# Head of the Strassen stage in written order, and one decay product behind the next projection

## The chip, the core and the metric

One core of a Trainium2 chip runs the whole program: TensorE (PE, with its weight loads as PEld), VectorE (DVE), ScalarE (ACT), GpSimd (POOL) and SyncE (SP), which issues the transfers. The metric is the device time of one execution in microseconds (us), lower is better, as the median of several runs.

## The reference

Two layers; each is a SwiGLU block, a mixer, and a second SwiGLU block, every one between two RMSNorms with a residual. There are 512 tokens, a width of 1024, a hidden width of 2816, all in float32.

```python
def swiglu_ffn(h, w_gate, w_up, w_down):
    return (jax.nn.silu(h @ w_gate) * (h @ w_up)) @ w_down

# inside the mixer, gated linear attention in chunks of 64 tokens
decay_to_end = lax.cumsum(la_c, axis=2, reverse=True) - la_c
chunk_decay = jnp.exp(jnp.sum(la_c, axis=2))
k_dec = to_chunks(k) * jnp.exp(decay_to_end)
```

The rest of the mixer (stick-breaking attention, a causal convolution, sigmoid gates, two output projections) is not touched by the change.

## The kernel before

**Precision.** A float32 operand is split into a high part (`whi`, `xh`: a rounded copy by ACT) and a low part (`wlo`, `xl`: the difference by DVE); a product is three matmuls, high by high, high by low and low by high. `split` and `load_w` do that for activations and weights. The order in which these helpers' instructions stand on ACT and DVE is left to a planner, which places each as soon as it expects it to be ready. `keep_in_program_order` pins an instruction behind the one written before it for the same engine. All matmuls and transposes are pinned.

**One SwiGLU block** (`ffn`, four times in the program: two in each layer) has 22 tiles of 128 hidden columns. Tiles 0 and 1 are computed token by token: `pf` holds gate and up of one block of 128 tokens, `ht` is their product, and four `ht` are transposed (`pth`) into `hid[0]` and `hid[1]`. Tile 2 is the classical tile: `pg` and `pu` are 24 matmuls each, then `hid[2]` is silu(`pg`) (ACT, L477) times `pu` (DVE, L478). Tiles 3 to 21 are computed by `block_tiles`, called the Strassen stage here: gate and up columns are taken together as a 2 by 2 block matrix, with seven products per tile instead of eight.

**Forms and operands.** The seven products take activations in seven forms: B11, B21, B22 are slices of `xh`/`xl`; T1 to T4 are sums over tokens that `Forms.arrive` makes and `Forms.finish` splits (L306 to L312). The weight side of each product is an operand that `prepare(g)` makes from the raw tile of the Strassen stage (sums on DVE, a copy to `whi` on ACT, and `low` for `wlo` on DVE, mostly for two products at a time). `product(g)` issues its 12 matmuls into bank A, B or C; `taken` and `summed` take the results out. `AHEAD = 6`: the loop runs from g = -6, and prepares the operand of product g + 6 in round g. Everything that `block_tiles` puts on ACT and DVE is pinned.

**Order before.** `ffn` writes the token tiles, `pg`, the transposes, all of `forms.finish()`, `pu`, the two instructions of `hid[2]` and then the whole of `block_tiles`. So the first pinned DVE instruction of `prepare(0)` stands behind the `hid[2]` product L478.

**Buffers.** `whi`/`wlo` have five slots; `raw` three tiles, each with room for one Strassen tile or two ordinary loads (`spare` holds the free half). The tag "s" has 14 slots: four `ht`, and four each for the split T3, T2 and T1 in the head.

**Decay.** `gla_decay` is a generator that the mixer moves on between convolution projections (`conv_in`, two projections each, `pa` and `pgl`). Its last part issues the `plam` matmuls, the exponential `lam` on ACT (L733), and for j = 0, 1 a product `pd` of 128x512 into one of the two banks of tag "pa". `plam` and the first `pd` fill these banks; the second `pd` takes the bank of `plam`.

Of the kernel before, what the change touches and what calls it, by code (L numbers as in the profile page):

```python
# [13 lines left out]
P = 128  # L14
# [27 lines left out]
def kernel(  # L42
# [21 lines left out]

    def mm(*a, **k):
        tc.keep_in_program_order(nc.tensor.matmul(*a, **k))  # L66

    def transpose(*a):
        tc.keep_in_program_order(nc.tensor.transpose(*a))
# [206 lines left out]
    class Forms:  # L276
# [24 lines left out]
                for j, n in enumerate(("T3", "T4")):  # L301
                    nc.vector.tensor_tensor(self.raw[n][c][:, :, tok], t2, first[j][:, k], op=ALU.add)

        def finish(self):
            for n, tag in (("T3", "s"), ("T2", "s"), ("T1", "s"), ("T4", "b")):
                hi = [slot(n + "h", F32R, tag).rearrange("p (k t) -> p k t", k=2) for c in range(2)]  # L306
                lo = [slot(n + "l", F32R, tag).rearrange("p (k t) -> p k t", k=2) for c in range(2)]
                for c in range(2):
                    split(hi[c], lo[c], self.raw[n][c])
                self.parts[n] = [(hi[k // 2][:, k % 2], lo[k // 2][:, k % 2]) for k in range(4)]  # L310
            for n, k0, t0 in (("B11", 0, 0), ("B21", 4, 0), ("B22", 4, 256)):
                self.parts[n] = [(xh[:, k0 + k, t0:t0 + 256], xl[:, k0 + k, t0:t0 + 256]) for k in range(4)]  # L312

    H0, H1 = slice(0, 256), slice(256, 512)

# [2 lines left out]
    PLACES = (0, 1, 0, 2, 4, 3, 2)  # L318
    AHEAD = 6

    def block_tiles(w0, w1, fs, forms, hid):

        pin = tc.keep_in_program_order
        copy = lambda o, i: pin(nc.scalar.copy(o, i))  # L324
        silu = lambda o, i: pin(nc.scalar.activation(o, i, AF.Silu))
        tt = lambda o, a, b, op: pin(nc.vector.tensor_tensor(o, a, b, op=op))  # L326
        add = lambda o, a, b: tt(o, a, b, ALU.add)
        sub = lambda o, a, b: tt(o, a, b, ALU.subtract)
        n = 7 * len(fs)
        raw, banks, cps, ring = {}, {}, {}, {}  # L330

        def load(u):
            r = wp.tile([P, 5, 512], F32, tag="raw", name="raw", bufs=3)
            for w, q0 in ((w0, 0), (w1, 1)):
                for j in range(2):
                    nc.sync.dma_start(r[:, q0 + 2 * j].rearrange("p (k c) -> p k c", c=P),
                                      w[j * 512:(j + 1) * 512, fs[u] * P:(fs[u] + 1) * P]
                                      .rearrange("(k p) c -> p k c", p=P))
            raw[u] = r

        def low(g0, g1):

            hi, lo = ring[g0 // 2]
            q0, q1 = PLACES[g0 % 7], PLACES[g1 % 7]
            r, h = raw[g0 // 7], g0 % 2
            if g0 == g1:
                sub(lo[:, h], r[:, q0], hi[:, h].bitcast(F32))
            elif q0 < q1:
                sub(lo, r[:, q0:q1 + 1:q1 - q0], hi.bitcast(F32))
            else:  # L350
                sub(lo[:, ::-1], r[:, q1:q0 + 1:q0 - q1], hi[:, ::-1].bitcast(F32))

        def prepare(g):

            u, j = divmod(g, 7)
            r = raw[u]
            if j == 0:
                add(r[:, 4], r[:, 1], r[:, 3])
                add(r[:, 1], r[:, 1], r[:, 0])
            if j == 2:  # L360
                add(r[:, 0], r[:, 4], r[:, 0])
            if j == 5:
                add(r[:, 2], r[:, 2], r[:, 0])
            if g % 2 == 0:
                ring[g // 2] = [wp.tile([P, 1024], F32R, tag=t, name=t).rearrange("p (f c) -> p f c", f=2)
                                for t in ("whi", "wlo")]
            copy(ring[g // 2][0][:, g % 2], r[:, PLACES[j]])
            if g % 2 and j:
                low(g - 1, g)
            elif g % 2 or j == 6:  # L370
                low(g, g)

        def product(g):
            u, j = divmod(g, 7)
            name, b = PRODUCTS[j]
            if j == 0:
                banks[u] = [bank(x) for x in "ABC"]
                cps[u] = gp.tile([P, D], F32, tag="g", name="cp")
            ps = banks[u][b][:, H0]
            hi, lo = (t[:, g % 2].rearrange("p (k c) -> p k c", c=P) for t in ring[g // 2])  # L380
            first = j in (0, 1, 3)
            for k, (fh, fl) in enumerate(forms.parts[name]):
                for m, (a, b_) in enumerate(((hi, fh), (hi, fl), (lo, fh))):
                    mm(ps, a[:, k], b_, start=(first and k == 0 and m == 0), stop=False, skip_group_check=True)

        def parts(u):
            cp = cps[u]
            return [cp[:, x * 256:(x + 1) * 256] for x in range(4)], hid[fs[u]], banks[u]

        def taken(g):  # L390

            u, j = divmod(g, 7)
            (p1, p7, u2, u4), h, (A, B, C) = parts(u)
            if j == 0:
                copy(p1, A[:, H0])
            if j == 1:
                copy(p7, C[:, H0])
            if j == 2:
                copy(u2, A[:, H0])
            if j == 4:  # L400
                copy(u4, A[:, H0])
            if j == 6:
                silu(h[:, H0], h[:, H0])
                silu(h[:, H1], A[:, H0])

        def summed(g):

            u, j = divmod(g, 7)
            (p1, p7, u2, u4), h, (A, B, C) = parts(u)
            if j == 3:  # L410
                add(h[:, H0], B[:, H0], p1)
            if j == 5:
                sub(u2, C[:, H0], u2)
                sub(u4, p7, u4)
            if j == 6:
                tt(h, cps[u][:, 512:1024], h, ALU.mult)

        for g in range(-AHEAD, n + 1):
            f = g + AHEAD
            if f % 7 == 0 and f < n:  # L420
                if f == 0:
                    load(0)
                if f // 7 + 1 < len(fs):
                    load(f // 7 + 1)
            if 0 < g:
                taken(g - 1)
            if 0 <= g < n:
                product(g)
            if f < n:
                prepare(f)  # L430
            if 0 < g:
                summed(g - 1)
# [8 lines left out]
    def ffn(wg, wu, wd, weights, forms, arrive, finish, upcoming, early, late, begin):  # L441

        if begin is None:
            wgt, wut = weights
        else:
            wgt = load_kcols(wg, 0, 256)
            begin(0)
            wut = load_kcols(wu, 0, 256)
            begin(1)
            arrive[0]()  # L450
        hk = []
        for i in range(NT):
            pf = bank("pf", "pb")
            mm_tok(pf[:, 0:256], i, wgt)
            if i + 1 < NT:
                arrive[i + 1]()
            mm_tok(pf[:, 256:512], i, wut, first=False)
            h = slot("ht", tag="s")
            nc.scalar.activation(h[:, 0:256], pf[:, 0:256], AF.Silu)
            nc.vector.tensor_tensor(h[:, 0:256], pf[:, 256:512], h[:, 0:256], op=ALU.mult)  # L460
            hk.append(h)
        hid = [None] * NF

        def turn(f):
            pt = bank("pth", "pa")
            for i in range(NT):
                transpose(pt[:, i * P:(i + 1) * P], hk[i][:, f * P:(f + 1) * P], ident)
            hid[f] = slot("hid", tag="q")
            nc.scalar.copy(hid[f], pt)

        pg = proj_cols(wg, 2 * P, "pg")
        turn(0)
        turn(1)
        forms.finish()
        pu = proj_cols(wu, 2 * P, "pu")
        hid[2] = slot("hid")
        nc.scalar.activation(hid[2], pg, AF.Silu)  # L477
        nc.vector.tensor_tensor(hid[2], pu, hid[2], op=ALU.mult)  # L478
        spare.clear()
        for f in range(3, NF):  # L480
            hid[f] = slot("hid", tag="t" if f < 18 else "q")
        block_tiles(wg, wu, list(range(3, NF)), forms, hid)
        late()

        def stat(f):
            sh, sl = slot("sh", F32R, "s"), slot("sl", F32R, "s")
            split(sh, sl, hid[f])
            return sh, sl

        return out_proj(wd, NF, stat, TAIL, finish, upcoming, early)  # L490


    def mixer(l, wv, arrive, finish, upcoming, early):
# [138 lines left out]
        ys = []  # L632
        taps = []

        def conv_in(c):
            pa = proj_cols(W, C_A + c * P, "pa")
            pg = proj_cols(W, C_G + c * P, "pgl")
            sg = slot("sgl", tag="s")
            nc.scalar.activation(sg, pg, AF.Sigmoid)
# [62 lines left out]
        def gla_decay(lrt):  # L702
# [31 lines left out]
            for j in range(2):  # L734
# [2 lines left out]
                e = slot("ge")  # L737
                nc.scalar.activation(e, pd, AF.Exp)
                nc.vector.tensor_tensor(gk[j], gk[j], e, op=ALU.mult)
            yield  # L740

        def gla_q():
            for c in range(2):
# [59 lines left out]
        conv_in(2)  # L803
        next(decay[0])
        conv_taps(10)
        conv_in(3)
        wr = load_kcols(W, C_GR, 512)
        conv_taps(4)

# [267 lines left out]
```

## Time and profile before

| | before |
|---|---|
| median of 3 runs | 2400.56 us (2398.08 to 2402.35) |
| profiled execution, own time | 2397.77 us |
| its span, first to last instruction | 2396.1 us |
| mean granted TensorE clock | 0.993 |
| PE busy | 2360.0 us (98%) |
| DVE / ACT / POOL busy | 1631.2 / 1118.0 / 175.9 us |

The profile is one execution. A matmul's end is modelled, so the intervals between starts are safer than durations. "Idle before" a row is the time for which its engine stood still, and the name behind the arrow is what ended it. The granted clock is 1.00 at 2.4 GHz and 0.50 at 1.2 GHz.

### The profile page before, as it was taken

The numbers are of one execution on the slowest core, as the hardware profiler recorded it, in microseconds if no ns is written. First come the engines' busy times: TensorE is split into PE (matmuls) and PEld (weight loads), VectorE is DVE, ScalarE is ACT, GpSimd is POOL, SyncE is SP. The second block draws the span as 40 slices with busy tenths as digits, with TensorE's granted clock in tenths as the row PEclk, the third lists the DMA queues.
The fourth block names the chain that finished last, engine by engine and source line by source line (L and its number), as shares of the span: only waits on it lengthen the run. The fifth ranks groups of instructions, "written<-read, shape, count | busy, mean of one in ns | idle before, by whom it ended". The sixth has DMA issues, their size and how long they took to land.

```text
span 2396.1 us, 35810 instructions
## 1 busy us (share of the span) xinstructions
PE 2360.0 (98%) x14264; PEld 2104.1 (88%) x14264; DVE 1631.2 (68%) x2329; ACT 1118.0 (47%) x2148; POOL 175.9 (7%) x287
## 2 busy tenths in 40 slices
PE   7999999999999999999999999999999999999998
PEld 7999888887888889998889998888878888899987
DVE  6888436858965378884378884378599644788833
ACT  5555425644323355563355563366333334455622
POOL 0000001201011100000000000012010211000000
PEclk9999999999999999999999999999999999999999
DMA  5333323231333223334223333241313332333421
GB/s 151 106 107 106 141 88 99 70 93 53 107 88 105 80 66 106 104 103 146 76 71 107 106 113 134 71 116 53 110 53 106 88 104 64 88 106 105 134 101 40
DMA packets 307159, 231.74 MB, mean 97 GB/s; under 512 B 11722, under 2 KB 284140, under 8 KB 306992
## 3 DMA queue, kind: packets, MB, share of 16 engines
q1 hardware_dynamic: 306992, 229.46, 32.2%
q8 instruction: 111, 1.82, 0.3%
q14 instruction: 56, 0.46, 0.1%
HBM read 227.32 MB, written 2.10 MB: 96 GB/s over the span
## 4 chain that ended last, share of the span: by engine, by line
PE 96%; DVE 2%; ACT 1%; issue 0%; POOL 0%; DMA 0%; SPq 0%; DVEq 0%; POOLq 0%; ACTq 0%
PE o L66 23%; PE A L66 18%; PE gate L66 11%; PE C L66 9%; PE pb L66 5%; PE B L66 5%; PE pf L66 4%; PE pa L66 2%; PE gr L66 2%; PE q L66 2%; PE gv L66 2%; PE k L66 2%; PE pgl L66 2%; PE pv L66 2%; PE pu L66 1%; PE gk L66 1%
## 5 line engine op out<-in xcount | busy, mean ns | idle before, releaser
L106 DVE TENSOR_TENSOR wlo<-raw,whi 128x1024 fp32r<-128x1024 f32 (+1 forms) x266 | 332.9, 1257 | 227.2 <-ACT whi L105 220.0
L105 ACT CAST whi<-raw 128x1024 fp32r<-128x1024 f32 (+1 forms) x266 | 278.1, 1046 | 391.8 <-PE gate L66 122.6
L326 DVE TENSOR_TENSOR wlo<-raw,whi 128x1024 fp32r<-128x1024 f32 (+1 forms) x304 | 330.5, 1088 | 117.7 <-ACT whi L324 117.5
L324 ACT CAST whi<-raw 128x512 fp32r<-128x512 f32 x532 | 314.2, 619 | 187.3 <-DVE raw L326 187.3
L66 PE MATMUL o<-whi,sh 128*128 128x512 f32 x704 | 274.2, 389 | 0.0
L66 PE MATMUL o<-wlo,sh 128*128 128x512 f32 x704 | 273.9, 389 | 0.0
L66 PE MATMUL o<-whi,sl 128*128 128x512 f32 x704 | 273.9, 389 | 0.0
L326 DVE TENSOR_TENSOR raw<-raw 128x512 f32<-128x512 f32 x304 | 209.2, 688 | 6.6
L106 DVE TENSOR_TENSOR sl<-hid,sh 128x512 fp32r<-128x512 f32 x88 | 60.0, 689 | 192.3 <-ACT sh L105 192.3
L66 PE MATMUL A<-xh,wlo 128*128 128x256 f32 x608 | 174.8, 288 | 15.1 <-DVE wlo L326 15.1
L66 PE MATMUL A<-xl,whi 128*128 128x256 f32 x608 | 173.6, 286 | 0.0
L66 PE MATMUL A<-xh,whi 128*128 128x256 f32 x608 | 173.6, 286 | 0.0
L667 DVE SCALAR_TENSOR_TENSOR y<-u,cw,y 128x511 f32<-128x511 f32 (+14 forms) x240 | 164.1, 743 | 0.0
L105 ACT CAST sh<-hid 128x512 fp32r<-128x512 f32 x88 | 54.4, 622 | 230.5 <-PE o L66 230.5
L66 PEld LDWEIGHTS o<-whi,sl 128*128 128x128 f32 x704 | 132.1, 188 | 27.4
L66 PEld LDWEIGHTS o<-wlo,sh 128*128 128x128 f32 x704 | 132.2, 188 | 27.3
L66 PEld LDWEIGHTS o<-whi,sh 128*128 128x128 f32 x704 | 132.2, 188 | 27.2
L66 PE MATMUL gate<-xh,whi 128*128 128x512 f32 x384 | 151.3, 394 | 0.0
L66 PE MATMUL gate<-xl,whi 128*128 128x512 f32 x384 | 149.6, 390 | 0.0
L66 PE MATMUL gate<-xh,wlo 128*128 128x512 f32 x384 | 149.5, 389 | 0.0
L193 POOL TENSOR_TENSOR rs<-ms,mhalf 128x1 f32<-128x1 f32 x48 | 30.9, 644 | 1480.2 <-DVE ms L191 1480.2
L66 PEld LDWEIGHTS A<-xh,wlo 128*128 128x128 f32 x608 | 118.8, 195 | 15.9 <-DVE wlo L326 15.9
(278 smaller groups left out, 6241.4 us busy)
## 6 DMA issues: line engine op xcount, KB each, us to landing
raw<-in_w_in_dram SPq DMA_DIRECT2D x108, 512.0 KB, 4.2
raw<-in_ffn_w_down_dram SPq DMA_DIRECT2D x88, 512.0 KB, 4.4
raw<-in_ffn_w_gate_dram SPq DMA_DIRECT2D x152, 256.0 KB, 3.4
raw<-in_ffn_w_up_dram SPq DMA_DIRECT2D x152, 256.0 KB, 4.5
raw<-in_w_branch_dram SPq DMA_DIRECT2D x24, 512.0 KB, 3.8
raw<-in_w_out_dram SPq DMA_DIRECT2D x16, 512.0 KB, 4.1
raw<-in_ffn_w_gate_dram SPq DMA_DIRECT2D x12, 512.0 KB, 5.4
raw<-in_ffn_w_up_dram SPq DMA_DIRECT2D x12, 512.0 KB, 4.0
```

What stands on the lines that cost most here:

```text
L66: tc.keep_in_program_order(nc.tensor.matmul(*a, **k))
L105: nc.scalar.copy(hi, src)
L106: nc.vector.tensor_tensor(lo, src, hi.bitcast(F32), op=ALU.subtract)
L193: nc.gpsimd.tensor_tensor(rs, ms, mhalf[:, 0:1], op=ALU.pow)
L324: copy = lambda o, i: pin(nc.scalar.copy(o, i))
L326: tt = lambda o, a, b, op: pin(nc.vector.tensor_tensor(o, a, b, op=op))
L667: nc.vector.scalar_tensor_tensor(y[:, back:], u[:, :S - back], cw[:, c, j:j + 1], y[:, back:], op0=ALU.mult, op1=ALU.add)
```

## The change

The forms, the token sums and the classical tile are no longer finished ahead of `block_tiles`, but inside its rounds, by a function `between(g)` that is called at the start of each round. `finish` splits one form at a time, with pinned instructions. The last `ht`, the loads of the classical tile's weights, `pg`, `pth` and `pu` keep their order on PE. In the mixer the generator yields after each `pd`, and `conv_in(3)` moves it on between its two projections.

```diff
-        def finish(self):
-            for n, tag in (("T3", "s"), ("T2", "s"), ("T1", "s"), ("T4", "b")):
...
-                for c in range(2):
-                    split(hi[c], lo[c], self.raw[n][c])
+        def finish(self, n):
+            tag = "b" if n == "T4" else "s"
...
+            for c in range(2):
+                pinned(nc.scalar.copy(hi[c], self.raw[n][c]))
+            for c in range(2):
+                pinned(nc.vector.tensor_tensor(lo[c], self.raw[n][c], hi[c].bitcast(F32), op=ALU.subtract))
...
         for g in range(-AHEAD, n + 1):
+            between(g)
             f = g + AHEAD
...
-        pg = proj_cols(wg, 2 * P, "pg")
-        turn(0)
-        turn(1)
-        forms.finish()
-        pu = proj_cols(wu, 2 * P, "pu")
-        hid[2] = slot("hid")
-        nc.scalar.activation(hid[2], pg, AF.Silu)
-        nc.vector.tensor_tensor(hid[2], pu, hid[2], op=ALU.mult)
+        def between(g):
+            if g == -6:
+                sides.append(load_cols(wg, 2 * P))
+                forms.finish("T3")
+            if g == -5:
+                silu_up(NT - 1, pf)
+                sides.append(load_cols(wu, 2 * P))
+                pg = bank("pg")
+                mm_cols(pg, *sides[0])
+                for f in range(2):
+                    pt = bank("pth", "pa")
+                    for i in range(NT):
+                        transpose(pt[:, i * P:(i + 1) * P], hk[i][:, f * P:(f + 1) * P], ident)
+                    pts.append(pt)
+                pu = bank("pu")
+                mm_cols(pu, *sides[1])
+                pts.extend((pg, pu))
+            if g == -4:
+                forms.finish("T2")
+            if g == -2:
+                forms.finish("T1")
+                for f in range(2):
+                    hid[f] = slot("hid", tag="q")
+                    pinned(nc.scalar.copy(hid[f], pts[f]))
+            if g == -1:
+                hid[2] = slot("hid")
+                pinned(nc.scalar.activation(hid[2], pts[2], AF.Silu))
+            if g == 0:
+                forms.finish("T4")
+            if g == 1:
+                pinned(nc.vector.tensor_tensor(hid[2], pts[3], hid[2], op=ALU.mult))
...
-        block_tiles(wg, wu, list(range(3, NF)), forms, hid)
+        sides = []
+        spare.clear()
+        block_tiles(wg, wu, list(range(3, NF)), forms, hid, between)
...
-        def conv_in(c):
+        def conv_in(c, mid=None):
             pa = proj_cols(W, C_A + c * P, "pa")
+            if mid is not None:
+                next(mid)
             pg = proj_cols(W, C_G + c * P, "pgl")
...
                 nc.vector.tensor_tensor(gk[j], gk[j], e, op=ALU.mult)
-            yield
+                yield
...
-        conv_in(3)
+        conv_in(3, decay[0])
```

## Rows read from the trace of the kernel before

**Rows 1.** The page: busy us (share) xinstructions, and granted clock in 40 slices.
```profile
PE 2360.0 (98%) x14264; PEld 2104.1 (88%) x14264; DVE 1631.2 (68%) x2329; ACT 1118.0 (47%) x2148; POOL 175.9 (7%) x287
...
PEclk9999999999999999999999999999999999999999
```

**Rows 2.** Waits of PE over the span: us in total, times, longest.
```profile
PE A L66 <- DVE wlo L326: 15.1, 4, 3.8
...
PE pd L66 <- ACT lam L733: 3.3, 2, 1.7
```

**Rows 3.** Chain that ended last, first head: start us, us, what.
```profile
46.60 5.47 PE pu L66 x24
...
52.10 0.04 DVE hid L478
...
52.70 0.69 DVE raw L326
...
54.80 1.24 DVE wlo L326
...
56.08 2.50 PE A L66 x10
```

**Rows 4.** Windows: six products in four heads, then steady: length, PE busy (x), clock, DMA.
```profile
51.90:66.92 15.02, 11.24 (x74) 0.77 0.24 67
884.89:899.92 15.03, 11.25 (x73) 0.77 0.25 70
1241.54:1256.56 15.02, 10.80 (x73) 0.89 0.24 69
2071.69:2087.08 15.39, 11.61 (x74) 0.78 0.24 69
77.00:85.64 8.64, 8.64 (x75) 1.00 0.39 108
```

**Rows 5.** Windows right behind the first head's wait and the first decay's.
```profile
56.08:61.27 5.19, 5.19 (x24) 0.50 0.00 0
...
553.83:559.61 5.78, 5.78 (x12) 0.50 0.00 0
```

**Rows 6.** Timeline of DVE, first head: start us, us, instruction, count, [idle before <-releaser].
```profile
34.38 1.42 DVE L302 TENSOR_TENSOR T<-T,xr 128x256 f32<-128x256 f32 x4
...
41.22 1.29 DVE L106 TENSOR_TENSOR T3l<-T,T3h 128x512 fp32r<-128x512 f32 x2
...
47.88 0.69 DVE L106 TENSOR_TENSOR T1l<-T,T1h 128x512 fp32r<-128x512 f32 x1 [3.56 <-ACT T1h L105]
```

**Rows 7.** Timeline of ACT, first head.
```profile
46.26 1.07 ACT L469 COPY hid<-pth 128x512 f32<-128x512 f32 x2
...
47.72 0.64 ACT L324 CAST whi<-raw 128x512 fp32r<-128x512 f32 x1
```

**Rows 8.** Timeline of SP, second SwiGLU: transfers of the first and third Strassen tiles.
```profile
849.59 0.92 SPq L336 DMA_DIRECT2D raw<-in_ffn_w_gate_dram  x2
...
871.31 0.92 SPq L336 DMA_DIRECT2D raw<-in_ffn_w_gate_dram  x2
```

**Rows 9.** Timeline of PE around the first decay.
```profile
549.36 1.84 PE L66 MATMUL plam<-indic,gm 128*128 128x2 f32 x16
551.06 1.10 PE L66 MATMUL pd<-gm,strict 128*128 128x512 f32 x2
553.83 2.07 PE L66 MATMUL pd<-gm,strict 128*128 128x512 f32 x2 [1.67 <-ACT lam L733]
```

**Rows 10.** Chain that ended last, ACT's part of the first decay.
```profile
553.59 0.19 ACT lam L733
```

**Rows 11.** Windows: one `pa` projection, then both decays from `plam` to `pgl`.
```profile
538.33:543.92 5.59, 5.59 (x26) 1.00 0.75 189
549.36:562.98 13.62, 11.95 (x45) 0.75 0.00 0
1738.86:1749.78 10.92, 9.25 (x45) 1.00 0.00 0
```

More of the change, by code (lines that the diff above doesn't have):

```diff
@@ L66, in mm @@
         tc.keep_in_program_order(nc.tensor.matmul(*a, **k))
+    pinned = tc.keep_in_program_order
     def transpose(*a):
@@ L302, in arrive, with form @@
                     nc.vector.tensor_tensor(self.raw[n][c][:, :, tok], t2, first[j][:, k], op=ALU.add)
-        def finish(self):
-            for n, tag in (("T3", "s"), ("T2", "s"), ("T1", "s"), ("T4", "b")):
-                hi = [slot(n + "h", F32R, tag).rearrange("p (k t) -> p k t", k=2) for c in range(2)]
-                lo = [slot(n + "l", F32R, tag).rearrange("p (k t) -> p k t", k=2) for c in range(2)]
-                for c in range(2):
-                    split(hi[c], lo[c], self.raw[n][c])
-                self.parts[n] = [(hi[k // 2][:, k % 2], lo[k // 2][:, k % 2]) for k in range(4)]
-            for n, k0, t0 in (("B11", 0, 0), ("B21", 4, 0), ("B22", 4, 256)):
+        def finish(self, n):
+            tag = "b" if n == "T4" else "s"
+            hi = [slot(n + "h", F32R, tag).rearrange("p (k t) -> p k t", k=2) for c in range(2)]
+            lo = [slot(n + "l", F32R, tag).rearrange("p (k t) -> p k t", k=2) for c in range(2)]
+            for c in range(2):
+                pinned(nc.scalar.copy(hi[c], self.raw[n][c]))
+            for c in range(2):
+                pinned(nc.vector.tensor_tensor(lo[c], self.raw[n][c], hi[c].bitcast(F32), op=ALU.subtract))
+            self.parts[n] = [(hi[k // 2][:, k % 2], lo[k // 2][:, k % 2]) for k in range(4)]
+        def form(self, n):
+            if n not in self.parts:
+                k0, t0 = {"B11": (0, 0), "B21": (4, 0), "B22": (4, 256)}[n]
                 self.parts[n] = [(xh[:, k0 + k, t0:t0 + 256], xl[:, k0 + k, t0:t0 + 256]) for k in range(4)]
+            return self.parts[n]
     H0, H1 = slice(0, 256), slice(256, 512)
@@ L319, with block_tiles @@
     AHEAD = 6
-    def block_tiles(w0, w1, fs, forms, hid):
-        pin = tc.keep_in_program_order
+    def block_tiles(w0, w1, fs, forms, hid, between):
+        pin = pinned
         copy = lambda o, i: pin(nc.scalar.copy(o, i))
@@ L381, in product @@
             first = j in (0, 1, 3)
-            for k, (fh, fl) in enumerate(forms.parts[name]):
+            for k, (fh, fl) in enumerate(forms.form(name)):
                 for m, (a, b_) in enumerate(((hi, fh), (hi, fl), (lo, fh))):
@@ L451, in ffn, with silu_up @@
         hk = []
+        hid = [None] * NF
+        def silu_up(i, pf):
+            h = slot("ht", tag="s")
+            nc.scalar.activation(h[:, 0:256], pf[:, 0:256], AF.Silu)
+            nc.vector.tensor_tensor(h[:, 0:256], pf[:, 256:512], h[:, 0:256], op=ALU.mult)
+            hk.append(h)
         for i in range(NT):
@@ L457, in ffn @@
             mm_tok(pf[:, 256:512], i, wut, first=False)
[L458 to L469, printed above, removed]
@@ L471, in ffn @@
-        pg = proj_cols(wg, 2 * P, "pg")
-        turn(0)
-        turn(1)
-        forms.finish()
-        pu = proj_cols(wu, 2 * P, "pu")
-        hid[2] = slot("hid")
-        nc.scalar.activation(hid[2], pg, AF.Silu)
-        nc.vector.tensor_tensor(hid[2], pu, hid[2], op=ALU.mult)
+            if i + 1 < NT:
+                silu_up(i, pf)
+        pts = []
+        def between(g):
[29 more added lines that the diff above has]
+                pinned(nc.vector.tensor_tensor(hid[2], pts[3], hid[2], op=ALU.mult))
+                for f in range(3, NF):
+                    hid[f] = slot("hid", tag="t" if f < 18 else "q")
@@ L479, in ffn @@
+        sides = []
         spare.clear()
-        for f in range(3, NF):
-            hid[f] = slot("hid", tag="t" if f < 18 else "q")
-        block_tiles(wg, wu, list(range(3, NF)), forms, hid)
+        block_tiles(wg, wu, list(range(3, NF)), forms, hid, between)
         late()
```

## The prediction

> **What bounds the kernel now.** I read the page first: PE is busy for 2360.0 us of the 2396.1 us span, and its granted clock shows 9 tenths or more in every slice, so slow stretches are short [rows 1]. Little can be won outside PE, and what can is where PE stands still or runs slow. So the second view is the waits of PE. Its two rows with several waits are 15.1 us in 4 waits for `wlo` and 3.3 us in 2 waits for `lam` [rows 2]; four is the number of SwiGLU blocks, two that of mixers. The third view, the chain of waits, shows what the first kind is made of. `pu` ends at 52.07; only then DVE can make the product `hid[2]` (52.10), and the sums on `raw` (52.70), the copy and `wlo` (54.80) follow one after the other; bank A resumes at 56.08 [rows 3]. The sums do not read `pu`. Their tile was loaded long before (in the second block its transfers went out at 849.59, 35 us ahead of the head at 884.89 [rows 4, 8]); they stand behind the `hid[2]` product because they are pinned to DVE's order. Fourth, I asked for windows: six products of 12 matmuls of 256 columns last 8.64 us in the steady stretch (6 x 1.44), but about 15 us in each head [rows 4], and the clock right behind the wait is 0.50, that is 1.2 GHz, after PE had stood still for 3.78 us [rows 5].
>
> **The change part by part: the heads.** No matmul is added or removed, and PE's order is kept. What leaves the path is the dependence of the first sums on `pu`. The price of a head is its window less 8.64: 15.02 - 8.64 = 6.38, then 6.39, 6.38 and 6.75, together 25.90 us [rows 4]. That holds the wait itself (4 x 3.78 = 15.1) and 10.8 us of slow clock and operands that come late behind it.
>
> What is late next? I put the new order on DVE, in times of the first head. T3 and T4 sums end at 34.38 + 1.42 = 35.8 [rows 6]. From then DVE has, in written order, T3l (1.29), two sums (0.7 each), the split of the `pu` weights (1.23), `low` of products 0 and 1 (1.23), T2l (1.29), a sum (0.7), `low` of 2 and 3 (1.23), the last `ht` (0.42): 8.8 us, durations of such instructions in the same timeline [rows 3, 6]. It would end near 44.6 if nothing held it; some 2 us go to waits for ACT's copies, so 47. `pu` ends at 52.07 [rows 3], so product 0 finds its operand some 5 us early or more.
>
> The next link is T1l. It needs two more slots of tag "s": four `ht`, eight for T3 and T2 and two for T1h are 14 of 14, so it waits for the transposes of `ht`. Before, the second T1l ran at 47.88, behind that same release, and the copies out of `pth` on ACT at 46.26 [rows 6, 7]. Behind T1l stand a sum and `low` of 4 and 5: 47.9 + 1.3 + 0.7 + 1.2 = 51.1. Product 4 starts at 51.9 + 4 x 1.44 = 57.7. Then T4l and `low` of 6: 51.1 + 2.0 = 53.1, against 60.5. So every operand has 6 us or more. ACT needs a copy of 0.6 us for each operand and form half, fewer than DVE's. I take the new wait at 0, with the full 25.9 us won; the cover is this lead, and if half of it were gone, the price is the second rival's.
>
> Of moved steps: the product `hid[2]` goes to round 1, behind `low` of 6, with nobody waiting for it until the output projection, a whole stage later. Its wait for `pu` at 52.07 is over by then; behind it in DVE's queue are the sums for product 7, due at 62. On SP, the `pu` weights are now written behind the loads of the first two Strassen tiles. In the second block, the first of these went out at 849.59 and the third, which waits for the `pu` split, at 871.31 [rows 8]; `pu`, which takes 5.5 us [rows 3], starts there at about 884.9 - 5.5 = 879.4 [rows 4]. Landing takes about 4 us, so even behind the second load the weights come in time: 0. The 16 form instructions, sums and copies are the same in number: 0.
>
> **The decay.** After `plam` and the first `pd` at 551.06, the second `pd` waits 1.67 us, because its bank is the one that ACT must read for `lam` first, at 553.59 [rows 9, 10]. Now 24 matmuls of `pa`, 5.59 us, stand between [rows 11]: from about 552.1 to 557.7, 4 us after `lam`. The wait goes: 2 x 1.67 = 3.34. In the first layer the clock fell to 0.50 for 5.78 us behind it [rows 5], in the second it did not: 13.62 - 10.92 = 2.70 more [rows 11]. Together 6.04 us. The second exponential and the product on `gk` come about 5 us later; `gk` of the second half is first read in the fifth chunk, behind four gate projections of 24 matmuls: 0. Built up instead from the parts (1.70 for `plam`, two `pd` of 1.03, 5.59), the pair of windows should be 9.35 each, a gain of 5.84, so the two ways agree within 0.2.
>
> **Sum.** 25.90 + 6.04 = 31.9 us. Against the profiled execution, 2397.77 - 31.9 = 2365.9. That execution was the shortest seen, 2.8 under the median, so the median after should be 2400.56 - 31.9 = 2368.6; I say 2368.5.
>
> **The rivals.**
> *The decay gives nothing back.* If the planner puts the late exponential where ACT is in the way of the next projection, 6.04 is lost again: 2374.6. For: ACT switches function tables around `lam`. Against: `lam` itself takes 0.19 us [rows 10], an exponential on 512 columns about as long as any copy of 512, 0.6 us, and the projection behind has its weights in five slots, loaded ahead. 5%.
> *Half the lead is gone.* One wait stays in each head, at product 2 or 4, of the size of the decay's: 1.67 and 2.70 for the clock, 4 x 4.37 = 17.5 kept: 2386.1. For: T1l hangs on a slot. Against: the 6 us computed above. 5%.
> *The wait was for a buffer.* The same wait of 3.78 us stands in four heads; were it a wait for a free `whi` slot, order would not help and only the decay would gain: 2400.56 - 6.04 = 2394.5. Against: the first operand's copy had its slot at 47.72, before `pu` ended [rows 7], and DVE ran its sums without a break from `hid[2]` on. The Trainium skill, "Perfetto Trace Analysis", section "Identifying Performance Opportunities", says that the same gap repeating on the engine that should be saturated can mean that there is no room for the next tile; here the rows speak for queue order instead. 5%.
> *Slower: DVE paces the head.* A pair of products takes PE 2.88 us, while DVE needs about 3.2 for it now that a form's split stands in the same chain (1.29 + 0.7 + 1.23). With the lead it does not matter. If the chain started only as `pu` ends, which takes a first link held by something that `pu` releases, each head would lose the old 6.4 and the four form splits, 4 x 1.29 = 5.2, which before lay in DVE's idle time: 4 x 5.2 - 6.0 = 14.8 slower, 2415. It turns slower than before when more than 1.5 us of splits a head lands behind `pu`. Against: T3's sums are there 16 us earlier. 3%.
>
> **How the numbers follow.** The forecast has 82%. Its own range is 2363 (the profile's 2365.9 less the 2.5 us between median and fastest run) to about 2373. With the first rival the range goes to 2378 and leaves out some 13%. A measurement can tell about 0.2%, 4.8 us, from no change. Forecast and the first two rivals are faster (92%); of the buffer case, at 6 us, 2 in 5 parts count as faster and 3 as the same; so 94, 3 and 3%.
>
> **What would show it.** After: no wait of bank A for `wlo` at a head, and windows of 8.6 us for the first six products at clock 1.00; the `hid[2]` product on DVE behind the seventh operand; T1l right behind the transposes; no wait for `lam`, and about 9.4 us from `plam` to `pgl` in both layers. Wrong would be a wait inside the first block, at product 2, 4 or 6, with DVE's T2l or T1l just ahead of it, or a late `pu`.

## The result and the profile after

The kernel after takes 2366.84 us (median of 4 runs, 2366.42 to 2367.24), the kernel before 2399.32 (4 runs, 2397.08 to 2402.35) beside it: a ratio of 0.9864 with a 95% interval of 0.9847 to 0.9881, 32.5 us or 1.4% less. Forecast were 2368.5 us, with a range of 2363 to 2378. The profiled executions differ by 2397.77 - 2367.24 = 30.5 us, their spans by 2396.1 - 2365.5 = 30.6, against the 31.9 of the prediction's sum.

The page of the kernel after, span and busy time:

```profile
span 2365.5 us, 35797 instructions
...
PE 2347.7 (99%) x14264; PEld 2094.3 (89%) x14264; DVE 1629.1 (69%) x2329; ACT 1117.9 (47%) x2148; POOL 181.1 (8%) x287
```

PE has the same 14264 matmuls, and is busy for 12.3 us less than in [rows 1]: that part of the gain had gone to slow clock, the rest to standing still. The waits of PE after (us in total, times, longest):

```profile
PE pt L71 <- DVE hn L210: 7.7, 1, 7.7
PE pf L66 <- ACT xh L107: 1.6, 1, 1.6
PE gate L66 <- DVE wlo L108: 1.3, 2, 0.6
PE pf L66 <- DVE xl L108: 0.8, 2, 0.6
```

Both rows of [rows 2] are gone. `pt` and `pf` wait at the start of the program, as before. One row is new: the first `gate` projection of each mixer waits 0.6 us for `wlo`.

The windows of the first six products in the four heads (length, PE busy (x instructions), granted clock, DMA share, GB/s), which answer to [rows 4]:

```profile
52.48:61.11 8.63, 8.63 (x74) 1.00 0.44 123
875.17:883.81 8.64, 8.64 (x73) 1.00 0.43 123
1225.13:1233.77 8.64, 8.64 (x73) 1.00 0.44 121
2047.90:2056.54 8.64, 8.64 (x74) 1.00 0.43 121
```

Each head runs at the steady pace from its first matmul and at full clock: 60.46 - 34.55 = 25.91 us less. For the decay I take windows from the start of `plam` to the start of `pu`, the first matmuls of the linear attention, behind the last projection of the convolution (there the moved `pd` is inside both times). First the kernel before, then after:

```profile
549.36:568.51 19.15, 17.48 (x69) 0.82 0.19 56
1738.86:1755.31 16.45, 14.78 (x69) 1.00 0.12 33
```

```profile
543.35:557.92 14.57, 14.57 (x69) 1.00 0.00 1
1716.06:1730.64 14.58, 14.58 (x70) 1.00 0.01 2
```

That is 35.60 - 29.15 = 6.45 us less. The rest of the balance: the two new waits at the gate, 1.3 us of standing, and the first head, which starts at 52.48 instead of 51.90, 0.6 later. The latter is no effect of the change: it arises between 16.9 and 18.3 us, where PE issued 14 matmuls in the execution before and 8 in the one after, and in a second execution of the kernel after the first head starts at 51.99. 25.91 + 6.45 - 1.26 - 0.58 = 30.5.

Last, the timeline of DVE and of ACT in the first head after (start us, us, instruction, count, [idle before <-releaser]):

```profile
40.30 1.22 DVE L336 TENSOR_TENSOR wlo<-raw,whi 128x1024 fp32r<-128x1024 f32 x1
...
46.96 1.29 DVE L314 TENSOR_TENSOR T1l<-T,T1h 128x512 fp32r<-128x512 f32 x2 [0.83 <-PE pth L71]
...
49.41 1.22 DVE L336 TENSOR_TENSOR wlo<-raw,whi 128x1024 fp32r<-128x1024 f32 x1 [0.56 <-ACT whi L334]
...
51.76 0.68 DVE L336 TENSOR_TENSOR wlo<-raw,whi 128x512 fp32r<-128x512 f32 x1
...
52.96 0.68 DVE L513 TENSOR_TENSOR hid<-pu,hid 128x512 f32<-128x512 f32 x1
```

```profile
50.30 0.64 ACT L334 CAST whi<-raw 128x512 fp32r<-128x512 f32 x1
50.82 0.64 ACT L107 CAST sh<-hid 128x512 fp32r<-128x512 f32 x1
54.11 0.37 ACT L334 COPY cp<-A 128x256 f32<-128x256 f32 x1 [2.65 <-PE A L66]
...
56.99 0.37 ACT L334 COPY cp<-A 128x256 f32<-128x256 f32 x1 [0.55 <-PE A L66]
```

`low` of products 0 and 1 is done at 41.5, 11 us ahead of product 0 at 52.48; the product with `pu` runs behind the seventh operand and holds up nobody. The rows to remember are the last two, ACT's copies of products 0 and 2 out of bank A. ACT stands idle for 2.65 us until PE has filled the bank for the first, and for 0.55 us before the second. Products 2 and 4, which need the emptied bank, start at 55.35 and 58.23, 0.87 us behind the end of each copy.

### The profile page after: what moved, and what is told of

The parts are those of the page before. It is cut to its first block, busy times and chain, and to the rows that moved or that the text cites. A ratio compares the mean times of both kernels' runs of the same rounds, so it can differ in the third digit from the quotient of the medians.

```text
span 2365.5 us, 35797 instructions
## 1 busy us (share of the span) xinstructions
PE 2347.7 (99%) x14264; PEld 2094.3 (89%) x14264; DVE 1629.1 (69%) x2329; ACT 1117.9 (47%) x2148; POOL 181.1 (8%) x287
## 3 DMA queue, kind: packets, MB, share of 16 engines
q1 hardware_dynamic: 306992, 229.46, 32.5%
## 5 line engine op out<-in xcount | busy, mean ns | idle before, releaser
L66 PEld LDWEIGHTS A<-xh,whi 128*128 128x128 f32 x608 | 116.7, 192 | 0.2
```

## The experiments

My theory: each head stood still only because its first sums stood behind the `hid[2]` product in DVE's order, and the new order has lead enough. The rivals: the forms have to be interleaved too; the wait was for a buffer; a wait stays inside the head. For the decay: the second `pd` waited for its bank. "Before" is the kernel before, run on the same chip as each experiment.

| kernel | median, us | runs from to | before |
|---|---|---|---|
| decay part alone | 2392.65 | 2391.98 to 2394.75 | 2398.44 |
| heads alone | 2372.47 | 2369.08 to 2373.71 | 2398.44 |
| before, `hid[2]` product moved alone | 2377.90 | 2376.12 to 2379.61 | 2398.44 |
| before, `pd` in other banks | 2393.98 | 2393.33 to 2394.42 | 2398.44 |
| after, `hid[2]` in round -3 | 2382.38 | 2382.01 to 2382.58 | 2399.50 |
| after, `hid[2]` in round -4 | 2398.31 | 2397.00 to 2399.39 | 2399.50 |
| after, all of tile 2 ahead of T3 | 2417.62 | 2415.99 to 2418.07 | 2399.50 |
| round -3, operands 5 and 6 later | 2389.88 | 2389.38 to 2391.57 | 2398.26 |
| `hid[2]` alone, operands 5 and 6 later | 2375.08 | 2374.79 to 2378.60 | 2398.26 |
| after, once more | 2366.73 | 2366.33 to 2367.08 | 2400.26 |
| after, four taps later | 2365.19 | 2364.95 to 2365.76 | 2399.50 |
| after, two taps later | 2365.47 | 2365.16 to 2365.55 | 2400.26 |

**Each part alone.** The two halves of the diff were applied one at a time.

> Only the decay part of the change, on the kernel before. By the sum of the prediction: no wait of PE for lam, 6.0 us less than the 2399.3 of before, 2393.3, perhaps 1.3 more if the two waits of 0.6 us for wlo at the first gate, which the trace of after shows, belong to this part (2394.6). Rival, the decay gives nothing back: 2399.

> Only the heads, the decay as before. By the sum: 25.9 us less, 2373.4, no wait of bank A, and the two waits for lam still there. If the two waits for wlo at the first gate belong to the heads, they are seen here too. Rival, the two parts overlap in what they win (a shared slow clock): then this run is under 2370.

Measured: 5.8 us less for the decay (ratio 0.9979, 0.9969 to 0.9988) and 26.0 less for the heads (0.9890, 0.9873 to 0.9906). Together 31.8, against 32.5 for both in one kernel: they add up, with no shared part that the two medians could show. The waits of PE, decay part alone, then heads alone:

```profile
PE A L66 <- DVE wlo L326: 15.1, 4, 3.8
...
PE gate L66 <- DVE wlo L106: 1.3, 2, 0.6
```

```profile
PE pd L66 <- ACT lam L770: 3.3, 2, 1.7
```

The new wait at the gate belongs to the decay part.

**The bank of `pd`.** This edit moves no instruction in the written program:

```diff
-                pd = bank("pd", "pa")
+                pd = bank("pd")
```

> The kernel before with the pd products in banks of the six of tag pb instead of the two of tag pa; order untouched. If the second pd waited for the bank that lam reads, the wait goes without any move: 2393.3 (6.0 less), possibly 2394.6. Rival, pd waits for ACT for another reason (ACT's exponential behind it): 2399 and the wait is still in the trace.

Measured: 4.5 us less (0.9983, 0.9974 to 0.9993), between the two values expected. PE has no wait for `lam` any more, and the waits of 0.6 us at the gate are there:

```profile
PE A L66 <- DVE wlo L326: 15.1, 4, 3.8
...
PE gate L66 <- DVE wlo L106: 1.3, 2, 0.6
```

So the second `pd` waited for the bank that ACT had yet to read, and a free bank takes the same wait away as the move. Its median is 1.3 us above that of the move. In the two profiled executions this is not in the stretches with the decay: from the first matmul of an output projection through a mixer to the next head, bank and move take 631.37 and 631.50 us in the first layer, 631.21 and 631.24 in the second. Where the 1.3 us come from stays open.

**One instruction moved.** In the kernel before, the product L478 alone is pinned in round 1 of the Strassen stage:

```diff
-        nc.vector.tensor_tensor(hid[2], pu, hid[2], op=ALU.mult)
+        def between(g):
+            if g == 1:
+                tc.keep_in_program_order(nc.vector.tensor_tensor(hid[2], pu, hid[2], op=ALU.mult))
...
         for g in range(-AHEAD, n + 1):
+            between(g)
```

> The kernel before with one instruction moved: the hid[2] product goes from ahead of the Strassen stage into its round 1, pinned there; forms, transposes and silu stay as before. If the wait is DVE's queue behind that product alone, all 25.9 us of the heads are won: 2373.4 (2372 to 2375), as with the whole new head. Rival, the forms must be interleaved and pinned too: a wait of PE stays at product 2 or 4 behind the form splits, 2 to 4 us a head, 2382 to 2390.

Measured: 20.5 us less, 5.4 short of the heads alone, and between the two ranges expected. No wait of bank A for `wlo` is left, which settles the question of the buffer: order alone removes it. But there is another wait, at the products that the rival named, though smaller and not the wait for form splits that it gave as the cause (waits of PE, then ACT's timeline in the first head):

```profile
PE A L66 <- ACT cp L324: 4.4, 8, 0.6
```

```profile
54.14 0.62 ACT L324 CAST whi<-raw 128x512 fp32r<-128x512 f32 x1 [0.97 <-DVE raw L326]
54.66 0.37 ACT L324 COPY cp<-A 128x256 f32<-128x256 f32 x1
```

Products 0, 2, 4 and 6 share bank A. Product 2 may not start until ACT has copied product 0 out, and that copy stands in ACT's pinned order behind the copies of the operands up to round 0, one of which waits for a sum on DVE. PE waits twice in each head, 0.56 us at product 2 and 0.53 at product 4. The forms' place matters, but through ACT's way out of the banks, not through operands that come too late for PE.

**How much lead there is.** Silu and product of `hid[2]` were moved forward in the new order, to round -3 and to round -4; `+` lines stand in `between`:

```diff
+            if g == -3:
+                hid[2] = slot("hid")
+                pinned(nc.scalar.activation(hid[2], pts[2], AF.Silu))
+                pinned(nc.vector.tensor_tensor(hid[2], pts[3], hid[2], op=ALU.mult))
```

> The kernel after with silu and the hid[2] product moved from rounds -1 and 1 to round -3, so that from there on DVE's pinned work stands behind pu (52.6 us in the first head). Lead theory, with durations of the trace of after: low of 2 and 3 by 54.5 (due 55.6), T1l and a sum by 56.4, low of 4 and 5 by 57.6 (due 58.5): no wait, 2366.8 within 1 us. Rival, any wait for pu ahead of the operands costs: at least 2 us a head, 2375 or more.

> The same, moved to round -4, ahead of T2's split. Lead theory: T2l, a sum, two copies and low of 2 and 3 end at 57.6 where product 2 wants it at 55.6, then low of 4 and 5 at 61.3 where product 4 wants it at 60.5: about 3 us a head, 12 in all, 2379; with a slow clock behind these waits up to 2390. Rival, the lead is still enough: 2366.8.

Measured: 15.5 us more than the kernel after for round -3, where I expected nothing, and 31.5 more for round -4, where I expected 12 to 23. Both expectations counted when `wlo` is due and forgot the copies out of bank A. In round -3, waits of PE, then DVE and ACT in the first head:

```profile
PE A L66 <- ACT cp L334: 7.8, 5, 1.8
```

```profile
52.05 0.69 DVE L505 TENSOR_TENSOR hid<-pu,hid 128x512 f32<-128x512 f32 x1 [9.05 <-PE pu L66]
...
55.00 0.69 DVE L336 TENSOR_TENSOR raw<-raw 128x512 f32<-128x512 f32 x1
```

```profile
55.72 0.62 ACT L334 CAST whi<-raw 128x512 fp32r<-128x512 f32 x1 [4.35 <-DVE raw L336]
56.24 0.36 ACT L334 COPY cp<-A 128x256 f32<-128x256 f32 x1
```

DVE stands still for 9 us before `pu`, then makes `low`, T1l and at 55.00 the sum for product 6 (it is written with operand 5, in round -1). ACT waits for it with the copy of operand 6, and only behind that takes product 0 out of bank A, at 56.24; product 2 starts at 56.66 instead of 54.8. In round -4 the same copy is at 61.01, and each head waits 5.8 us.

To test that reading, operands 5 and 6 were prepared (the expectation calls the copy that waits that of product 5; it is that of 6, and the edit moves both), and T4 split, behind the first copy out of bank A, with DVE still 9 us behind `pu`:

```diff
             if 0 < g:
                 taken(g - 1)
...
+            if g == 1:
+                prepare(5)
+                forms.finish("T4")
+                prepare(6)
-            if f < n:
+            if f < n and g not in (-1, 0):
                 prepare(f)
```

> The kernel with the hid[2] product in round -3 (2382.4), and the operands of products 5 and 6 and T4's split written after the first copy out of bank A instead of ahead of it. If the waits of that kernel come from ACT, whose copy out of A stands behind the copy for product 5 (which waits for a sum on DVE, which stands behind pu), product 2 no longer waits, while DVE still stands behind pu for 9 us: 2368 (2366 to 2371). Rival, it is DVE's lateness itself that PE pays: no better than 2382.

Measured: 2389.88, 7.5 us worse, so the time came out against my number and as the rival had it. The trace says what happened (waits of PE; ACT in the first head):

```profile
PE A L66 <- ACT cp L334: 14.9, 4, 3.7
```

```profile
53.97 0.37 ACT L334 COPY cp<-A 128x256 f32<-128x256 f32 x1 [4.13 <-PE A L66]
...
61.02 0.62 ACT L334 CAST whi<-raw 128x512 fp32r<-128x512 f32 x1 [3.29 <-DVE raw L336]
61.54 0.36 ACT L334 COPY cp<-A 128x256 f32<-128x256 f32 x1
```

The first copy now runs as soon as PE has filled bank A, and product 2 no longer waits, as the reading says. But the copy of product 2 out of A stands, as before, behind an operand's copy that waits for DVE: 61.54 here, 60.99 in round -3, in a head that began 0.55 us earlier. Product 4 starts no sooner, and the wait for it is one piece of 3.7 us. What it lost besides is clock. Windows between and behind the waits, round -3 first, then this kernel:

```profile
57.80:61.20 3.40, 3.40 (x17) 0.50 0.36 104
```

```profile
62.20:65.60 3.40, 3.40 (x18) 0.50 0.60 163
```

In round -3 the slow stretch lies ahead of product 4, which has to wait until 61.4 in any case; here it lies behind, and is paid in full. So ACT's order is shown as the cause of the wait at product 2; but PE pays for DVE's lateness all the same, and moving two operands only moves the place at which it reaches PE. My number had looked no further than the first copy.

The same rewriting on the kernel with one instruction moved, where DVE is late by less:

> The kernel with one instruction moved (2377.9), with the same rewriting of products 5 and 6 behind the first copy out of A. If its two waits of 0.56 and 0.53 us a head are ACT's copies out of A behind operand copies, the first goes, and the second at least in part: 2373 to 2375, near the whole new head alone (2372.5). Rival, the split of the forms ahead of the operands is what is left: 2378.

Measured: 2375.08, at the upper edge of the range expected and 2.8 us better, but the runs of the two kernels overlap (2374.79 to 2378.60 against 2376.12 to 2379.61). The wait at product 2 is gone, as expected; the one at product 4 has grown from 0.53 to 1.2 us, and the waits together have not shrunk (4.4 us without the rewriting):

```profile
PE A L66 <- ACT cp L324: 4.9, 4, 1.2
```

From the first matmul of the Strassen stage to the first of the output projection, a block takes 192.98 us here, 193.1 without the rewriting and 191.5 with the heads alone, so the rewriting won some 0.5 us in all four heads. Most of the difference between the two profiled executions is a slow clock behind the wait for `lam`, which the edit does not touch. In the kernel without the rewriting, windows of 5.78 us from the second `pd` on show it in both layers; here they run at 1.00 (shown in the last section):

```profile
548.49:554.27 5.78, 5.78 (x16) 0.71 0.00 0
1727.33:1733.11 5.78, 5.78 (x12) 0.52 0.00 0
```

That the median came near my range is luck, then. In the heads the rewriting shows only that the wait at product 2 was ACT's order, and that product 4 pays instead.

**The slower rival made real.** The last `ht`, `pg`, `pth`, `pu`, silu and product of `hid[2]` were all written in round -6, ahead of `forms.finish("T3")`, by moving these lines of `between` there.

> The slower rival of the prediction made real: the last ht, pg, transposes, pu, silu and the hid[2] product all written in round -6 ahead of T3's split, so that all operands and form splits stand behind pu on DVE. The prediction's price is 11.6 us a head: 2366.8 + 46.4 = 2413. Worked out link by link from the trace of after it is 5.0 + 1.6 + 0.9 us of waits and about 2.6 of slow clock, 10.1 a head: 2407. If form splits cost nothing in the chain it is the 6.4 of before: 2392.5.

Measured: 2417.62, above all three numbers: 50.8 more than the kernel after, 12.7 a head, and slower than before (1.0074, 1.0059 to 1.0089). Waits of PE:

```profile
PE A L66 <- DVE wlo L336: 20.2, 4, 5.1
PE A L66 <- ACT cp L334: 13.1, 4, 3.5
```

The first wait is the 5.0 us that was worked out link by link. The second is ACT's copy out of bank A again. The same instructions, with the same pins, are 33 us faster or 18 us slower than before by where the classical tile stands on ACT and DVE.

**The new wait at the gate.** On DVE, the split of the gate's weights stands behind convolution taps. The timeline of DVE and of PE after:

```profile
581.81 3.29 DVE L706 SCALAR_TENSOR_TENSOR y<-u,cw,y 128x493 f32<-128x493 f32 x5
585.02 2.34 DVE L108 TENSOR_TENSOR wlo<-raw,whi 128x1024 fp32r<-128x1024 f32 x2
```

```profile
587.42 0.50 PE L66 MATMUL gate<-xh,wlo 128*128 128x512 f32 x1 [0.63 <-DVE wlo L108]
```

The `conv_taps(4)` behind `wr` was changed to 0 and to 2; these taps are then done with the gates of the third branch.

> The kernel after with four convolution taps fewer in the mixer ahead of the gla gates (they are done later, ten with each gate of the third branch). If the new wait of 0.63 us for wlo at the first gate comes from taps that stand ahead of it on DVE, it goes in both layers: 1.3 us less, 2365.5. Rival, it hangs on ACT's copy or on the weights: 2366.8, wait unchanged.

> The kernel after once more, unchanged, to stand beside the next run on one chip: 2366.8. If the waits at the first gate are fixed by the order of the program, both are there again with 0.63 us; if they come by chance, they are not.

> The kernel after with two convolution taps fewer ahead of the gla gates, instead of four. A tap takes DVE about 0.65 us, the wait at the gate was 0.63 us: if taps ahead of wlo are its cause, one tap is about what it takes, so two should take the wait away as four did, 1.3 us less than the kernel after on this chip. Rival, the order around the gate changes only with more taps moved: wait unchanged, same time.

Measured: 2365.19 and 2365.47; on the chip of the latter the kernel after took 2366.73, with both waits in its trace at 0.63 us. So two taps are enough, and the gain is 1.3 us, with no overlap between the runs of the two kernels (2365.16 to 2365.55 against 2366.33 to 2367.08). With two taps moved, DVE in the first layer:

```profile
580.24 3.17 DVE L706 SCALAR_TENSOR_TENSOR y<-u,cw,y 128x493 f32<-128x493 f32 x4
583.33 2.35 DVE L108 TENSOR_TENSOR wlo<-raw,whi 128x1024 fp32r<-128x1024 f32 x2
```

The wait is gone from the waits of PE. These are the fastest kernels of the study, ahead of both that were given. Why the change brought the wait at all is less sure. The planner places unpinned instructions anew, and in the kernel after five taps stand directly ahead of the split, where before one stood there, with small work in between. That PE now comes to the gate sooner, with less time for the same taps, is argued, not separated from it.

## Why the prediction was right, and where it was not

**What bounds it, and the price of a head.** Right. 25.90 us were worked out from windows less 8.64 [rows 4]; the windows after give 25.91 against the same execution before, the part alone 26.0 in time. The premise that nothing but order held the sums stood the test of moving one instruction.

**The decay.** Right in kind, and 0.4 us small: 6.04 forecast, 6.45 by the windows, 5.8 (2.9 to 7.4) as a part alone, which has the 1.3 of the gate in it. The bank was the cause, as [rows 9, 10] were read. The 2.70 us for the clock were read from one execution, and the windows take the same one; others paid for a slow clock in both layers or in neither (last section), which by these prices makes 8.7 or 3.3 us. That 6.04 fits so well is in part luck.

**"What is late next?"** This step failed, though its answer, nothing, held for the kernel at hand. I listed when each `wlo` is due, found 6 us or more for every one, and wrote that ACT needs fewer copies than DVE. The operand of product 5 is indeed early. But tighter links were not in the list: the copies out of bank A. That of product 0 stands on ACT behind the copies of all operands up to round 0, and product 2 waits for it. Its lead was not 6 us but 2.65 + 0.87 = 3.5, and that of the copy of product 2, on which product 4 waits, 0.55 + 0.87 = 1.4. Two experiments whose expectations repeated that list missed by 15 us and by 8 us or more.

**What was moved "at 0".** True for the `hid[2]` product, the transfers and the forms. Not true for the mixer: I costed the moved exponential and product at 0 by who reads them, and did not ask what a re-planned DVE would put ahead of the gate's weights. That is 1.3 us of standing that the sum left out.

**The rivals.** The buffer is excluded by the moved instruction. "Half the lead is gone" did not come; a wait of its size does exist, through ACT and not through T1l, and costs 15.5 us at round -3 (17.5 was its price). The slower one was priced at 14.8 us above before, 2415, and came to 18.1 above, 2417.62, when it was made. Its price of 11.6 a head left out bank A; 12.7 were measured. Its turning point, 6.4 + 1.5 = 7.9 us lost a head, held: round -4 loses 31.5 / 4 = 7.9 and ties with before (0.9996, 0.9987 to 1.0005), as it must where the whole gain is 32. But it takes three form splits behind `pu` to get there, some 3.9 us, not 1.5.

**The number.** The sum from the profile, 2365.9, and from the median, 2368.6, lie on both sides of 2366.84. What missed is small and partly cancels: 0.4 too little for the decay, 1.3 of new waits not seen, and 0.6 of a later start by chance. The starting point missed too: before ran at 2399.32 beside the kernel after, not at 2400.56, and from there the sum gives 2367.4.

## What to carry to other kernels

When instructions are pinned on an in-order engine, look for one whose input comes late and ask what stands behind it that does not need it: here one 0.7 us product was worth 20 us. When you count lead in a new order, count what leaves the accumulators as well as what goes into the matmuls, on each engine; the copies out of a shared bank had the least slack, 1.4 us where the operands of the first seven products had 7 or more. And read the waits again after the gain: a planner that is free elsewhere will put something new ahead of something due.

## What was not expected of the hardware

The wait of 1.67 us for `lam` was followed by a slow clock in the first layer and not in the second [rows 5, 11]. Other executions with the same wait show other mixes. Windows of 5.78 us from the second `pd` on, both layers, of the heads alone and then of the kernel with one instruction and two operands moved:

```profile
547.67:553.45 5.78, 5.78 (x12) 0.52 0.00 0
1724.37:1730.15 5.78, 5.78 (x17) 0.74 0.00 0
```

```profile
548.71:554.49 5.78, 5.78 (x24) 1.00 0.00 0
1725.65:1731.43 5.78, 5.78 (x24) 1.00 0.00 0
```

In the same time PE issues 12, 17 or 24 matmuls. So one wait has no fixed price: here 1.67 us, or up to some 2.7 more. The runs of the kernel after lie within 0.8 us, those of before within 5.3. Waits alone do not spread the runs: the kernel with `hid[2]` in round -3, which waits in every head, lies within 0.6 us. But that kernel has no wait for `lam`. The four kernels that have it (before, heads alone, and the two with one instruction moved) spread by 3.49 us or more on every chip, those without it by 2.77 or less. Of the heads alone the two slower runs, both at 2373.7, have a mean granted clock of 0.997, the two faster, 2369.08 and 2371.26, one of 0.999. So the spread goes with the varying clock behind this wait; no run was made to single it out.
